# Whole 32-bit products in place of three split ones, in the projections and upward products of a second block

## The chip, the cores and the metric

The kernel runs on one core of one Trainium2 chip. The metric is the device time of one execution in microseconds (us), lower is better. Engines are named as in the profile: PE is the matrix engine (PEld its weight loads), DVE the vector engine, ACT the scalar engine, POOL is GpSimd, SP the engine whose queue issues most transfers.

## The reference, cut to what matters

One sequence of 256 tokens with 1024 channels goes through a first block (two layers of feed-forward, mixer, feed-forward), and then through a second block, whose mixer and experts follow. The change touches only the second block's mixer:

```python
h = modulate(rms_norm(x, g_pre_mix), shift, scale)      # 256 tokens x 1024 channels
z = h @ w_in + b_in                                     # 1024 -> 4736 columns: scans, attention, gates
y_att  = attention(...) @ w_up_att                      # 512 -> 1024
y_rwkv = scans(...)     @ w_up_rwkv                     # 512 -> 1024
x = x + norm((gate_a * y_att + gate_r * y_rwkv) @ w_out)
...                                                     # router, then 32 experts, four per token
```

All tensors are 32-bit floating point.

## The kernel before

The first block runs until about 1127 us of the span. The function `block2` is the second block up to the router, `experts` the rest. A framework orders the instructions of each engine at build time, from the order of the program and from planned durations; on the chip every engine keeps that order.

`norm` (L1370 to L1401) takes the two tiles of 128 tokens in turn: a factor per token, then eight products with a diagonal matrix (L1388) that scale and transpose at once, then DVE's modulation out of PSUM (L1391, tile `hch`), ACT's rounding into the float32r tile `hxH` (L1393), and DVE's remainder into `hxL` (L1394).

`Stream3` (L1135) brings the weights in 45 parts of 512 KB (37 for the projections, 8 for the upward products), 128 partitions by 1024 columns, read into two buffers `ws` (L1145). Each part is split in two halves of 512 columns: ACT rounds a half into `wh` (L1154), and the remainder `wl` is formed by DVE or, where the function `POOLED` says so, by GpSimd (L1156). Four pairs of halves are held, three halves ahead of use.

`pair` (L1403) forms 256 output columns from two parts: for each block of 128 columns and each 128 channels, three products of 128x128 weights with 256 tokens (L1412 to L1414), which are rounded weights with rounded input, rounded weights with the remainder of the input, and remainder of the weights with rounded input. There are 296 such triples. Five pairs come first (`first`: what the scans need). The other pairs (`fill`) are woven with the steps of the scans by the list `PACE`. A step of the scans in this stretch is either a feature step (products L260, L261, some twelve DVE operations from L264 to L296, then products L250 on `BKT`) or a part of the inverses of small triangular matrices (DVE, L320 to L340, 62 of them in a chain at L329 and L331, then products L346 to L356).

After them come attention, woven with the scans' chunks, then `rwkv_out`, then `up_att` and `up_rwkv`: `up` (L1566) is the same triple on the split outputs of attention (`atH`, `atL`, L1554 and L1555) and of the scans (`rwH`, `rwL`, L1623 and L1624), 64 triples at L1573 to L1575. The output product follows (L1666, whole 32-bit operands already), then router and experts. The experts' weights, 384 transfers of 1 MB (L1325), are read into 18 buffers.

Of the kernel before, what the change touches and what calls it, by code (L numbers as in the profile page):

```python
# [32 lines left out]
# buffers of the hidden units' chunks  # L33
NH = 4
N0 = 3
# steps of the scans beside each of the projections
PACE = [2] + [1, 2] * 4 + [1] * 6
# first ranks of an expert's groups of slots: 64, 32, 64, 64 and 32 of them
BASE = (0, 64, 96, 160, 224)
NWE, NWA = 18, 12  # L40
# subtiles of the last modulations read before the second mixer
PRE = 2
# subtiles of an expert in the order of their use: halves of the first product's rows one after the other, then the second's
ORDER = [0, 2, 4, 6, 1, 3, 5, 7, 8, 10, 9, 11]
# buffers of the second block's weights, of 512 KB
NRAW, NHI, AHEAD = 2, 4, 3


def POOLED(n, h):
    return (h or n % 2) and 10 <= n < 37 or n < 2  # L50
# columns of the per-layer channel pack of the first block
MC_CW, MC_CB, MC_G, MC_B, MC_LW, MC_LB, MC_BA, MC_BX, MC_LAM, MC_N = 0, 31, 32, 33, 34, 38, 39, 40, 41, 42
# columns of the channel pack of the second block
# [9 lines left out]
# subtiles of weights with a part of the split on GpSimd  # L63
# [3 lines left out]
def bc(ap, n, axis):  # L67
    """ap with a broadcast axis of n put in at position axis."""
    s = list(ap.shape)
    idx = [slice(None)] * len(s)  # L70
    idx.insert(axis, None)
    s.insert(axis, n)
    return ap[tuple(idx)].to_broadcast(s)
# [3 lines left out]
def program(ctx: ExitStack, tc: tile.TileContext, a, out, dbg=None, upto=99, only=None):  # L77
# [13 lines left out]
    # what is over before the experts  # L91
# [18 lines left out]
    def rstd_of(pool, var, eps, tag, more=None):  # L110
        """(var + more + eps) to the power of -1/2."""
# [12 lines left out]
    # ---------------------------------------------------------------- persistent  # L124
# [34 lines left out]
        # halves and sums of parameters that sit on the channels  # L159
# [11 lines left out]
    def normed_T(pool, bank, xt, mod, dst_h, dst_l):  # L171
        """rms norm, modulation and transposition of both token tiles, in two float32r parts."""
# [25 lines left out]
    def shifted(pads, ps, ch, dst):  # L198
        """Bias and token shift of a chunk, from PSUM to dst [P, 256]. ch counts the 15 shifted chunks."""
# [6 lines left out]
    def wkv(psb, k2, f, s_in, s_out, yT, kkn=None):  # L206
        """Chunked scans of both directions over chunks of 64 tokens, a piece at a time. Direction 0 keeps b on
        partitions 0-63 and k on 64-127 of what runs over tokens; direction 1 the other way round."""
# [17 lines left out]
        # k normalized  # L226
# [17 lines left out]
        def products(p, d):  # L244
            """Products of a (and r) with b and k inside a chunk."""
# [8 lines left out]
        for p in range(4):  # L254
            for d in range(2):
# [52 lines left out]
        # unit triangular inverses of the diagonal 32-blocks, one matrix on a partition  # L308
# [53 lines left out]
        # b, k and v with tokens on partitions  # L362
# [24 lines left out]
        # chunk after chunk, the heads in two halves  # L387
# [81 lines left out]
    def columns(ps, m, dst):  # L469
        """Modulations as columns: for each (tile, first of the two rows' groups) of dst."""  # L470
# [6 lines left out]
    def parts_of(split, dst):  # L477
        """What make_rows reads: two float32r parts of the rows that each (part, tile) of dst needs."""
# [9 lines left out]
    def make_rows(bank, parts, sel, dst):  # L488
        """Parts of x's modulation on all partitions, with the gains that go with them, for each (part, tile) of dst."""
# [8 lines left out]
    def context():  # L498
        """The modulation rows, and the keys, values and states of the context: three lists of steps that need
        no x, with the weights of each. The first two share what is in f."""  # L500
# [11 lines left out]
        def before():  # L512
            # the last part's first weights, for the norm behind the second mixer
# [61 lines left out]
        def mod_cols():  # L575
            # columns of shift and scale: 0 of x's first norm, 1 of the context's
# [76 lines left out]
    def weave(main, side, every):  # L653
        """The steps of main with one of side after every so many, and what is left of side at the end."""
# [41 lines left out]
    def proj(ps, w, j, n, xh, xl):  # L696
        """Chunk j of the n chunks of 128 columns of a subtile, [channels, tokens]."""
# [9 lines left out]
    def block1():  # L707
        KF, KM = 0.25 / ALPHA, 1.0 / ALPHA
        EPS = LN_EPS / (ALPHA * ALPHA)
        with ExitStack() as p1:  # L710
# [24 lines left out]
            def to_T(t, src):  # L735
                """x of a token tile, transposed, in two float32r parts."""
# [6 lines left out]
            def projx(ps, w, j, ts=slice(0, 2)):  # L743
                """Chunk j of the two of a subtile, of x's token tiles ts."""
# [61 lines left out]
            def rows(acc, w, h, l, first, last, ts=range(2)):  # L806
                """Products of a chunk of 128 rows of weights, [tokens, D]."""
# [8 lines left out]
            # ------------------------------------------------------------ gated unit  # L816
# [43 lines left out]
            # ------------------------------------------------------------ mixer  # L860
            def mixer(l):
# [3 lines left out]
                def consts_():  # L865
# [49 lines left out]
                def taps(g):  # L915
                    """The convolution of a half of the channels: first taps on GpSimd, the others on VectorE."""
# [180 lines left out]
            # ------------------------------------------------------------  # L1097
            st.xh, st.xl = parts("x")
            c0, c1, c2, before = context()
            # behind the ends of the units and mixers, what the norms there don't hold up  # L1100
# [33 lines left out]
    # =================================================================== phase 2  # L1134
    class Stream3:  # L1135
        """Parts of 512 KB of weights in the order of their use, read ahead and split into float32r parts,
        half a part at a time."""

        def __init__(self, raw, hl, ahead):
            self.raw, self.hl, self.ahead = raw, hl, ahead  # L1140
            self.srcs, self.f, self.t, self.n, self.i = [], {}, {}, 0, 0

        def load(self, i):
            self.f[i] = self.raw.tile([P, 1024], F32, name="ws", tag="ws")
            nc.sync.dma_start(self.f[i], self.srcs[i])  # L1145

        def ensure(self, i):
            while self.n < min(i + 1, 2 * len(self.srcs)):
                n, h = divmod(self.n, 2)
                if n not in self.f:  # L1150
                    self.load(n)
                f = self.f.pop(n)[:, 512 * h:512 * h + 512] if h else self.f[n][:, :512]
                hi = self.hl.tile([P, 512], F32R, name="wh", tag="wh")
                S.copy(hi, f)  # L1154
                lo = self.hl.tile([P, 512], F32R, name="wl", tag="wl")
# [4 lines left out]
        def next(self):  # L1160
            self.ensure(self.i + self.ahead)
            self.i += 1
            return self.t.pop(self.i - 1)
# [1115 lines left out]
```

## Time and profile before

| what | value |
|---|---|
| median of three runs | 2542.59 us (2541.45 to 2544.2) |
| span of the profiled execution, first to last instruction | 2534.9 us |
| own time of the profiled execution | not listed beyond its span; the median lies 7.7 us above it |
| mean granted PE clock | 0.945 of 2.4 GHz |
| PE, DVE, ACT, POOL busy | 2215.7, 1255.8, 766.8, 207.7 us |
| first block, second block to the router, experts | about 0 to 1127, 1127 to 1500, 1500 to 2535 us |

Busy times of PE count a matrix instruction from its start to its modelled end, so that instructions in a row overlap: the distance from one start to the next is what a stream of them costs.

### The profile page before, as it was taken

How to read it: one execution, taken by the hardware profiler on the slowest of the kernel's cores; microseconds unless marked ns; L12 is line 12 of the kernel's file. 1: busy time of each engine (PE TensorE's matmuls, PEld its weight loads, DVE VectorE, ACT ScalarE, POOL GpSimd, SP SyncE). 2: the span in 40 equal slices, each digit the busy share in tenths (PEclk: the TensorE clock that was granted, in tenths of full speed). 3: DMA queues.
4: the chain of work that ended last, by engine and by line, in shares of the span. 5: the costliest groups of instructions: out<-in, count | busy, mean ns of one | idle time of the engine just before them, and what ended most of it. 6: DMA issues, size and time to landing. Idle time of an engine off the chain costs nothing. (4 is left out here: it accounts for less than half of the span.)

```text
span 2534.9 us, 37664 instructions
## 1 busy us (share of the span) xinstructions
PE 2215.7 (87%) x15228; PEld 1562.4 (62%) x15228; DVE 1255.8 (50%) x2403; ACT 766.8 (30%) x1334; POOL 207.7 (8%) x198
## 2 busy tenths in 40 slices
PE   8999789999999789988879997887879778888787
PEld 7899668988997769978766743343333333333243
DVE  4667987886566975568985541111111112111112
ACT  3454354444444444446433311000101010000011
POOL 0001410001001410013430000000000000000000
PEclk9999899999999899999988998989999899999888
DMA  7655334444476355533320578969999999999983
GB/s 313 224 198 192 113 118 165 152 170 161 151 271 246 116 223 187 195 127 117 105 96 1 189 299 347 417 277 371 416 417 417 365 416 416 416 416 416 417 360 157
DMA packets 97081, 644.39 MB, mean 254 GB/s; under 512 B 11776, under 2 KB 13312, under 8 KB 23296
## 3 DMA queue, kind: packets, MB, share of 16 engines
q1 hardware_dynamic: 91152, 628.33, 63.7%
q10 hardware_dynamic: 5616, 11.75, 1.4%
q8 instruction: 213, 3.49, 0.6%
q14 instruction: 100, 0.82, 0.1%
HBM read 638.98 MB, written 1.05 MB: 252 GB/s over the span
## 5 line engine op out<-in xcount | busy, mean ns | idle before, releaser
L686 DVE TENSOR_TENSOR wl<-wst,wh 128x1024 fp32r<-128x1024 f32 x298 | 363.0, 1223 | 225.1 <-ACT wh L684 219.2
L751 PE MATMUL gu<-xh,wl 128*128 128x256 f32 x1632 | 458.2, 281 | 7.4 <-DVE wl L686 5.0
L749 PE MATMUL gu<-xh,wh 128*128 128x256 f32 x1632 | 459.9, 282 | 4.0 <-DVE yc L913 2.3
L750 PE MATMUL gu<-xl,wh 128*128 128x256 f32 x1632 | 458.2, 281 | 0.0
L684 ACT CAST wh<-wst 128x1024 fp32r<-128x1024 f32 x320 | 333.3, 1050 | 346.3 <-PE gu L750 188.8
L749 PEld LDWEIGHTS gu<-xh,wh 128*128 128x128 f32 x1632 | 311.1, 191 | 15.5 <-ACT xh L732 3.7
L751 PEld LDWEIGHTS gu<-xh,wl 128*128 128x128 f32 x1632 | 311.1, 191 | 12.0 <-DVE wl L686 6.6
L750 PEld LDWEIGHTS gu<-xl,wh 128*128 128x128 f32 x1632 | 311.2, 191 | 3.3 <-issue 0.3
L1805 PE MATMUL eg<-ew,eT 128*64 128x512 f32 x1024 | 267.9, 614 | 18.9 <-PEq L1988 12.1
L1849 DVE SCALAR_TENSOR_TENSOR eyl<-eg,gs,eyh 64x512 fp32r<-64x512 f32 x64 | 48.0, 750 | 358.4 <-ACT eyh L1848 358.4
L1866 PE MATMUL eg<-ew,xg 128*32 128x512 f32 x1408 | 184.2, 641 | 27.1 <-issue 20.4
L1805 PEld LDWEIGHTS eg<-ew,eT 128*64 128x64 f32 x1024 | 87.9, 140 | 170.4 <-issue 162.1
L1785 DVE TENSOR_SCALAR gg<-eg 128x256 f32<-128x256 f32 x42 | 17.8, 425 | 321.0 <-PE eg L1866 195.9
L1848 ACT ACTIVATE eyh<-eg,gs 64x512 fp32r<-64x512 f32 x64 | 43.7, 682 | 358.8 <-PE eg L1805 333.4
L1778 PE MATMUL eg<-ew,xg 128*64 128x512 f32 x640 | 147.1, 612 | 0.0
L1866 PEld LDWEIGHTS eg<-ew,xg 128*32 128x32 f32 x1408 | 47.7, 116 | 152.0 <-issue 135.4
L106 PE MATMUL acc<-wh,hl 128*128 128x512 f32 x352 | 138.8, 394 | 0.6 <-DVE hl L733 0.6
L105 PE MATMUL acc<-wl,hh 128*128 128x512 f32 x352 | 138.2, 393 | 0.0
L104 PE MATMUL acc<-wh,hh 128*128 128x512 f32 x352 | 138.0, 393 | 0.0
L1788 ACT ACTIVATE etu<-gg 128x256 f32<-128x256 f32 x45 | 18.8, 417 | 344.5 <-DVE gg L1785 324.9
L1761 PE MATMUL ms<-oh,hf 128*128 128x128 f32 (+2 forms) x608 | 85.4, 308 | 19.2 <-issue 13.4
L1414 PE MATMUL pj<-hxH,wl 128*128 128x256 f32 x296 | 88.9, 300 | 14.6 <-DVE wl L1156 13.2
(574 smaller groups left out, 3494.6 us busy)
## 6 DMA issues: line engine op xcount, KB each, us to landing
ew<-in_wexp SPq DMA_DIRECT2D x384, 1024.0 KB, 19.9
wst<-in_wgu SPq DMA_DIRECT2D x88, 1024.0 KB, 4.9
wst<-in_wd SPq DMA_DIRECT2D x44, 1024.0 KB, 4.9
wada<-in_wada SPq DMA_DIRECT2D x24, 1024.0 KB, 9.5
wst<-in_win SPq DMA_DIRECT2D x20, 1024.0 KB, 4.8
ws<-in_win SPq DMA_DIRECT2D x36, 512.0 KB, 3.6
wst<-in_wout SPq DMA_DIRECT2D x8, 1024.0 KB, 4.8
ws<-in_wup SPq DMA_DIRECT2D x8, 512.0 KB, 4.4
```

Of the source, the lines that this page charges most:

```text
L104: T.matmul(o, lh, rh, start=start, stop=False)
L105: T.matmul(o, lh, rl, start=False, stop=False)
L106: T.matmul(o, ll, rh, start=False, stop=stop)
L684: S.copy(hi, s_)
L686: (G if kind == SHARED and h else V).tensor_tensor(lo, s_, hi.bitcast(F32), op=ALU.subtract)
L749: T.matmul(o, h[:, c0:c0 + P], st.xh[:, ts, k], start=k == 0, stop=False)
L750: T.matmul(o, h[:, c0:c0 + P], st.xl[:, ts, k], start=False, stop=False)
L751: T.matmul(o, l[:, c0:c0 + P], st.xh[:, ts, k], start=False, stop=k == 7)
L1414: T.matmul(ps[:, j], l[:, c0:c0 + P], hh[:, kk], start=False, stop=kk == 7, skip_group_check=True)
L1778: T.matmul(ps[r][64 * j:64 * j + 64], xg[:, k], W(4 * r + 2 * j + q, k % 4), start=False, stop=k == 7, skip_group_check=True)
L1805: T.matmul(ps[c * two][64 * c:64 * c + 64], hT[:, r, j, b], W(8 + 2 * (c ^ flip) + k // 4, k % 4), start=k == 0, stop=k == 7)
L1866: T.matmul(ps[32 * b:32 * b + 32], xg[:, k], W(2 * b + q, k % 4), start=False, stop=k == 7, skip_group_check=True, tile_position=(0, 32 * b))
```

## The change

The splits are dropped. Weights are read into six buffers of 512 KB and used from there; the inputs are kept whole; each triple becomes one product with 32-bit operands. In `norm` every second chunk's modulation moves from DVE to ACT, and the results go straight into the input tile.

```diff
-NRAW, NHI, AHEAD = 2, 4, 3
-def POOLED(n, h):
-    return (h or n % 2) and 10 <= n < 37 or n < 2
+NRAW = 6
...
     class Stream3:
...
-                hi = self.hl.tile([P, 512], F32R, name="wh", tag="wh")
-                S.copy(hi, f)
-                lo = self.hl.tile([P, 512], F32R, name="wl", tag="wl")
-                (G if POOLED(n, h) else V).tensor_tensor(lo, f, hi.bitcast(F32), op=ALU.subtract)
-                self.t[self.n] = (hi, lo)
+        def load(self, n):
+            while self.n < min(n, len(self.srcs)):
+                self.t[self.n] = self.raw.tile([P, 1024], F32, name="ws", tag="ws")
+                nc.sync.dma_start(self.t[self.n], self.srcs[self.n])
                 self.n += 1
         def next(self):
-            self.ensure(self.i + self.ahead)
+            n, h = divmod(self.i, 2)
+            self.load(n + NRAW)
             self.i += 1
-            return self.t.pop(self.i - 1)
+            return self.t[n][:, 512 * h:512 * h + 512]
...
-        hh = hp.tile([P, 8, 256], F32R, name="hxH")
-        hl_ = hp.tile([P, 8, 256], F32R, name="hxL")
+        hx = hp.tile([P, 8, 256], F32, name="hx")
...
-                            V.tensor_scalar(f_[:, i], ps[:, i], modc[:, 0, 0, c:c + 1], modc[:, 0, 1, c:c + 1],
-                                            op0=ALU.mult, op1=ALU.add)
-                        S.copy(hh[:, cs, ts], f_)
-                        V.tensor_tensor(hl_[:, cs, ts], f_, hh[:, cs, ts].bitcast(F32), op=ALU.subtract)
+                            if i % 2:
+                                S.activation(hx[:, c, ts], ps[:, i], AF.Identity, scale=modc[:, 0, 0, c:c + 1], bias=modc[:, 0, 1, c:c + 1])
+                            else:
+                                V.tensor_scalar(hx[:, c, ts], ps[:, i], modc[:, 0, 0, c:c + 1], modc[:, 0, 1, c:c + 1],
+                                                op0=ALU.mult, op1=ALU.add)
...
-                        T.matmul(ps[:, j], h[:, c0:c0 + P], hh[:, kk], start=kk == j == 0, stop=False, skip_group_check=True)
-                        T.matmul(ps[:, j], h[:, c0:c0 + P], hl_[:, kk], start=False, stop=False, skip_group_check=True)
-                        T.matmul(ps[:, j], l[:, c0:c0 + P], hh[:, kk], start=False, stop=kk == 7, skip_group_check=True)
+                        T.matmul(ps[:, j], w[:, c0:c0 + P], hx[:, kk], start=kk == j == 0, stop=kk == 7, skip_group_check=True)
...
-                S.copy(at.h[:, :, ts], at.po)
-                V.tensor_tensor(at.l[:, :, ts], at.po, at.h[:, :, ts].bitcast(F32), op=ALU.subtract)
+                S.copy(at.x[:, :, ts], at.po)
...
-                        T.matmul(o[:, j], h[:, c0:c0 + P], yh[:, kk], start=kk == j == 0, stop=False, skip_group_check=True)
-                        T.matmul(o[:, j], h[:, c0:c0 + P], yl[:, kk], start=False, stop=False, skip_group_check=True)
-                        T.matmul(o[:, j], l[:, c0:c0 + P], yh[:, kk], start=False, stop=kk == 3, skip_group_check=True)
+                        T.matmul(o[:, j], w[:, c0:c0 + P], y[:, kk], start=kk == j == 0, stop=kk == 3, skip_group_check=True)
...
-                V.tensor_tensor(y, y, f.vT[:, c], op=ALU.mult)
-                S.copy(ro.h[:, c], y)
-                V.tensor_tensor(ro.l[:, c], y, ro.h[:, c].bitcast(F32), op=ALU.subtract)
+                V.tensor_tensor(ro.x[:, c], y, f.vT[:, c], op=ALU.mult)
...
-        for i in range(2):
-            st.load(i)
+        st.load(NRAW)
```

## Rows read from the trace of the kernel before

**Rows 1.** Stretches: length; busy PE, PEld, DVE, ACT, POOL; granted clock; DMA share; GB/s.

```profile
1134.30:1166.40 32.10, 31.88 (x241) 31.59 (x242) 25.31 (x38) 17.99 (x36) 7.38 (x5) 0.90 0.48 164
1166.40:1247.90 81.50, 68.34 (x500) 59.81 (x498) 73.01 (x144) 44.55 (x103) 36.22 (x34) 0.94 0.28 91
1247.90:1321.70 73.80, 55.18 (x595) 52.17 (x594) 64.65 (x93) 25.86 (x49) 27.25 (x23) 0.84 0.31 103
...
1413.90:1455.70 41.80, 38.88 (x278) 31.27 (x276) 24.57 (x44) 16.41 (x27) 1.27 (x3) 1.00 0.71 268
1455.70:1560.00 104.30, 91.73 (x423) 45.90 (x422) 35.19 (x116) 13.99 (x34) 4.70 (x6) 0.90 0.75 303
1560.00:2534.00 974.00, 791.37 (x4437) 342.38 (x4436) 172.88 (x496) 94.59 (x191) 7.65 (x23) 0.93 0.93 381
```

**Rows 2.** What SP's transfers waited for, 1120 to 1500 us (total, times, longest).

```profile
SPq L1325 <- PE wb L447: 99.7, 1, 99.7
...
SPq L1325 <- PE ac L1666: 16.7, 4, 5.7
```

**Rows 3.** What PE's instructions waited for, 1134 to 1322 us (total, times, longest).

```profile
PE wb L250 <- DVE BKT L292: 10.9, 6, 3.4
PE wb L346 <- DVE invL L339: 5.4, 1, 5.4
```

**Rows 4.** Groups of PE, 1166.4 to 1247.9 us, then 1247.9 to 1321.7 us.

```profile
L1414 PE MATMUL pj<-hxH,wl 128*128 128x256 f32 x108 | 31.4, 291 | 1.4 <-POOL wl L1156 1.4
...
L1414 PE MATMUL pj<-hxH,wl 128*128 128x256 f32 x109 | 34.0, 312 | 13.2 <-DVE wl L1156 13.2
```

**Rows 5.** Timeline of PE: third products of triples (start us, length us).

```profile
1139.96 0.41 PE L1414 MATMUL pj<-hxH,wl 128*128 128x256 f32 x1
...
1141.06 0.28 PE L1414 MATMUL pj<-hxH,wl 128*128 128x256 f32 x1
...
1142.13 0.28 PE L1414 MATMUL pj<-hxH,wl 128*128 128x256 f32 x1
```

**Rows 6.** Timeline of PE: whole 32-bit products, two instructions for each.

```profile
1360.06 0.59 PE L1561 MATMUL pj<-gl,g 128*128 128x256 f32 x2
...
1460.86 15.72 PE L1666 MATMUL ac<-ew,zg 128*128 128x512 f32 x36
```

**Rows 7.** Three source lines: all their durations in ns (min, median, max), first and last start.

```profile
L1561 PE MATMUL pj<-gl,g x8: 379/379/483, 1360.1 to 1394.5; 128*128 128x256 f32 x8
L1156 DVE TENSOR_TENSOR wl<-ws,wh x46: 673/685/2304, 1138.4 to 1451.8; 128x512 fp32r<-128x512 f32 x46
L291 DVE SCALAR_TENSOR_TENSOR BKT<-BKT,wk x16: 408/416/1517, 383.7 to 1245.9; 128x256 f32<-128x256 f32 x16
```

**Rows 8.** Timelines of DVE and of POOL, 1209 to 1213 us.

```profile
1209.99 1.52 DVE L291 SCALAR_TENSOR_TENSOR BKT<-BKT,wk 128x256 f32<-128x256 f32 x1
...
1209.93 4.12 POOL L1156 TENSOR_TENSOR wl<-ws,wh 128x512 fp32r<-128x512 f32 x3 [1.05 <-ACT wh L1154]
```

**Rows 9.** Groups of DVE, 1247.9 to 1321.7 us (busy us, mean ns).

```profile
L329 DVE TENSOR_TENSOR ttmp<-invL,invX 128x31 f32<-128x31 f32 (+15 forms) x31 | 18.4, 595 | 1.1
L331 DVE TENSOR_TENSOR invX<-invX,ttmp 128x31 f32<-128x31 f32 (+15 forms) x31 | 16.6, 535 | 0.9
```

**Rows 10.** The same operations in the first block's scan, 480 to 560 us.

```profile
L331 DVE TENSOR_TENSOR invX<-invX,ttmp 128x31 f32<-128x31 f32 (+15 forms) x31 | 10.6, 341 | 0.7
L329 DVE TENSOR_TENSOR ttmp<-invL,invX 128x31 f32<-128x31 f32 (+15 forms) x31 | 10.6, 341 | 0.7
```

**Rows 11.** Remainders (L1156) alone: busy on DVE, on POOL; clock, DMA share, GB/s.

```profile
1166.40:1247.90 81.50, 5.91 (x8) 28.80 (x20) 0.94 0.28 91
1247.90:1321.70 73.80, 7.55 (x11) 26.23 (x19) 0.84 0.31 103
```

**Rows 12.** Timeline of PE at the end of the norm.

```profile
1129.75 3.00 PE L1388 MATMUL wb<-dr,xf 128*128 128x128 f32 x16 [3.66 <-DVE dr L1381]
...
1134.30 0.58 PE L1412 MATMUL pj<-hxH,wh 128*128 128x256 f32 x1 [1.55 <-ACT hxH L1393]
```

More of the change, by code (lines that the diff above doesn't have):

```diff
@@ L1135, in program, with __init__ @@
     class Stream3:
[L1139 to L1152, printed above, removed]
-                hi = self.hl.tile([P, 512], F32R, name="wh", tag="wh")
-                S.copy(hi, f)
-                lo = self.hl.tile([P, 512], F32R, name="wl", tag="wl")
-                (G if POOLED(n, h) else V).tensor_tensor(lo, f, hi.bitcast(F32), op=ALU.subtract)
-                self.t[self.n] = (hi, lo)
+        def __init__(self, raw):
+            self.raw, self.srcs, self.t, self.n, self.i = raw, [], {}, 0, 0
+        def load(self, n):
+            while self.n < min(n, len(self.srcs)):
+                self.t[self.n] = self.raw.tile([P, 1024], F32, name="ws", tag="ws")
+                nc.sync.dma_start(self.t[self.n], self.srcs[self.n])
                 self.n += 1
         def next(self):
-            self.ensure(self.i + self.ahead)
+            n, h = divmod(self.i, 2)
+            self.load(n + NRAW)
             self.i += 1
-            return self.t.pop(self.i - 1)
+            return self.t[n][:, 512 * h:512 * h + 512]
     class Experts:
@@ L1344, in block2 @@
         kkn = yT = grow.rearrange("q (c t) -> q c t", c=4)
-        st = Stream3(ps_.enter_context(tpool(name="p2s", bufs=NRAW)), ps_.enter_context(tpool(name="p2l", bufs=NHI)), AHEAD)
+        st = Stream3(ps_.enter_context(tpool(name="p2s", bufs=NRAW)))
         psb = pa.enter_context(tpool(name="p2b", bufs=3, space=PSUM))
@@ L1383, in tile_ @@
                         ps = (psb if t else pjb).tile([P, 4, P], F32, name="wb" if t else "pj", tag="wb" if t else "pj")
-                        f_ = p.tile([P, 4, P], F32, name="hch", tag="hch", bufs=4)
-                        cs = slice(4 * q, 4 * q + 4)
                         for i in range(4):
@@ L1406, in pair @@
             for i in range(2 * n):
-                h, l = st.next()
+                w = st.next()
                 for j in range(n):
@@ L1499, in att_consts @@
             at.p = ap.enter_context(tpool(name="p2a", bufs=1))
-            at.h = at.p.tile([P, 4, 256], F32R, name="atH")
-            at.l = at.p.tile([P, 4, 256], F32R, name="atL")
+            at.x = at.p.tile([P, 4, 256], F32, name="atX")
             at.mask = at.p.tile([P, 2, P], F32, name="amask")
@@ L1564, in bonus, with up @@
             S.copy(f.vT[:, p], ps[:, 1])
-        def up(o, yh, yl):
+        def up(o, y):
             for i in range(2):
-                h, l = st.next()
+                w = st.next()
                 for j in range(2):
@@ L1572, in up @@
                         kk, c0 = 2 * i + k, 256 * k + P * j
-                        T.matmul(o[:, j], h[:, c0:c0 + P], yh[:, kk], start=kk == j == 0, stop=False, skip_group_check=True)
-                        T.matmul(o[:, j], h[:, c0:c0 + P], yl[:, kk], start=False, stop=False, skip_group_check=True)
-                        T.matmul(o[:, j], l[:, c0:c0 + P], yh[:, kk], start=False, stop=kk == 3, skip_group_check=True)
+                        T.matmul(o[:, j], w[:, c0:c0 + P], y[:, kk], start=kk == j == 0, stop=kk == 3, skip_group_check=True)
         def up_att(i):
             ps = pj()
-            up(ps, at.h, at.l)
+            up(ps, at.x)
             z = zg[:, 2 * i:2 * i + 2]
@@ L1594, in rwkv_out @@
             dump("yT", yT)
-            dump("atT", at.h.bitcast(F32))
+            dump("atT", at.x)
             mp = ro.p = ap.enter_context(tpool(name="p2r", bufs=1))
-            ro.h = mp.tile([P, 4, 256], F32R, name="rwH")
-            ro.l = mp.tile([P, 4, 256], F32R, name="rwL")
+            ro.x = mp.tile([P, 4, 256], F32, name="rwX")
             cs = [slice(2 * i, 2 * i + 2) for i in range(2)]
@@ L1621, in rwkv_out @@
                     V.scalar_tensor_tensor(y[:, j], y[:, j], at.lw[:, p:p + 1], f.bon[:, p], op0=ALU.mult, op1=ALU.add)
-                V.tensor_tensor(y, y, f.vT[:, c], op=ALU.mult)
-                S.copy(ro.h[:, c], y)
-                V.tensor_tensor(ro.l[:, c], y, ro.h[:, c].bitcast(F32), op=ALU.subtract)
-            dump("rwT", ro.h.bitcast(F32))
+                V.tensor_tensor(ro.x[:, c], y, f.vT[:, c], op=ALU.mult)
+            dump("rwT", ro.x)
         mg = Ctx()
@@ L1631, in up_rwkv @@
             ps = pj()
-            up(ps, ro.h, ro.l)
+            up(ps, ro.x)
             z, c = zg[:, 8 + 2 * i:10 + 2 * i], slice(2 * i, 2 * i + 2)
```

## The prediction

> **What bounds the kernel now.** I read the stretches first. In the experts, from 1560 us on, the transfers are busy 93% of the time and move 381 GB/s, while PE is busy for 791 of 974 us: that part is paced by the weights coming in. Between 1455.7 and 1560 us they run at 303 GB/s [rows 1]: their buffers are full and wait for use. The SP queue says the same. Its first transfer for the output product waits for the scans' last products (L447, 99.7 us), and later ones wait for buffers that the output product frees (L1666, 16.7 us) [rows 2]. So the experts' stream starts when the second block lets it, and has a length of its own. A microsecond gained or lost in the second block arrives at the end unchanged; this is the assumption under the sum.
>
> Inside the second block the change touches four stretches. I call them A (1134.3 to 1166.4 us, the first five pairs), B (to 1247.9, features of the scans beside pairs), C (to 1321.7, inverses beside pairs) and E (1413.9 to 1455.7, the upward products); between C and E lies attention. In A, PE is busy 31.9 of 32.1 us and is the bound. In B it is DVE, busy 73.0 of 81.5 us, with PE idle for 13.2; in C DVE again, 64.7 of 73.8, with PE idle for 18.6 [rows 1]. What ended PE's idle time is named: 10.9 us waited for `BKT`, DVE's last result of a feature step, 5.4 for the transposes after the inverses [rows 3], 13.2 for remainders from DVE and 1.4 for remainders from GpSimd [rows 4]. The reader should see that PE pays for DVE here, and that DVE is busy partly with work for PE.
>
> **What the change adds.** PE's price. At the high clock the third products of triples start at 1141.06 and, three triples on, at 1142.13: 0.357 us for a triple. Until 1140.8 us the clock stood at half, and the same product lasted 0.41 instead of 0.28 [rows 5]. A whole 32-bit product is two instructions. In the output product 36 of them with 512 columns take 15.72 us, 0.437 each; half the columns should take 0.218. L1561 has 256 columns: its two instructions take 0.59 us together, and one alone lasts 0.379, so 0.21 between their starts [rows 6, 7]. I take 0.43 us for a product of 256 columns, and 0.86 at half the clock (an estimate, twice that). Each triple replaced costs 0.43 - 0.357 = 0.07 us more: 296 in the projections 21 us, 64 upward 4.5 us.
>
> The Trainium skill (FP8 and Floating Point Precision, section TensorE Precision Notes) speaks against the change: it counts four passes through the array for a true 32-bit product, and a reduced form that truncates each operand. With passes of equal price that would be four thirds of the triple, 0.476 us, and 0.12 more for each of the 360 products, 43 us in place of 25. The rows of L1666 and L1561 lie below that, since a stream of float32r products costs more than its columns alone.
>
> **What it removes.** Of the 90 halves of weights, DVE forms 46 remainders at 0.685 us [rows 7], and GpSimd the rest. ACT, which rounds all of them, is busy less than 60% of A, B, C and E [rows 1], so what it saves gives nothing by itself. The remainders on GpSimd cost DVE as well: while three of them ran from 1209.93 to 1214.05 us, L291 took 1.52 us [rows 8], 1.1 more than its median of 0.416 [rows 7]. For the inverses the sum is clean, since the first block runs the same 62 operations without splits: 18.4 + 16.6 = 35.0 us here [rows 9] against 21.2 there [rows 10], so 13.8 us come back, beside 19 remainders on GpSimd. With the 11 remainders of its own, 7.6 us, DVE's 64.7 us in C fall to 43. In B 20 run on GpSimd [rows 11]; at 1.1 us each (L291's stretch) they cost DVE 22 us at most, at C's rate 14. Its own eight take 5.9 us, so DVE's 73 us fall to about 53.
>
> **The sum, stretch by stretch.**
> Norm and A. Now the transposing products end at 1132.75 us, and the first product starts at 1134.30, released by the rounding [rows 12]. Without rounding and with half of the evacuations on ACT the first channels are ready before the transposes end, so I start at 1132.8. The weights' first transfers still wait for the end of the first block, as before, and six buffers in place of two keep them ahead afterwards. The clock is at half until about 1140.8 [rows 5]: 8 us at 0.86 make 9.3 products, the other 70.7 at 0.43 take 30.4. A ends at 1171.2 instead of 1166.4: **+4.8**.
> B. PE was busy 68.3 us; 108 products [rows 4] add 7.6; the share of the lower clock (0.94 granted, 0.06 x 81.5 = 4.9 us lost, of which two thirds by its products) gives back 3.3: 72.6 us is the floor, above DVE's 53. Of the idle time 1.4 goes with its instruction; of the rest, 10.9 behind `BKT`, I keep 4, since every engine's order is fixed and a feature step still crosses three engines. 76.6 in place of 81.5: **-4.9**, between -8.9 (nothing kept) and +6.2 (all but the 1.4 kept, and the lower clock).
> C. PE was busy 55.2; 109 products add 7.6; the lower clock (0.84 granted, 11.8 us lost, of which I count half, since PE was partly idle then) gives back 5.9: 56.9. DVE's chain beside it is 43 us, then the last products and copies, so PE leads. I keep 4 of the 18.6 idle. 60.9 in place of 73.8: **-12.9**, between -16.9 and +7.6 (everything kept, the 13.2 now as waits on the inverses).
> Attention loses one remainder at its end, of the same size as L1156's 0.685 us: **-0.7**.
> E. 64 products add 4.5, and of the 2.9 idle [rows 1] I let 0.8 go, the waits for splits: **+3.7**. The rounding and remainder after the scans leave the path to `up_rwkv`, but the products of attention cover them.
> Together 4.8 - 4.9 - 12.9 - 0.7 + 3.7 = -10.0 us: a span of 2525 for 2534.9, and 2542.6 - 10.0 = 2532.6, rounded to **2532 us**, on the median, which lies 7.7 above the profiled span. The best sum, with nothing kept, is -18.0.
>
> **The rivals.**
> 1. *DVE's relief is half used.* PE keeps 16 us of its idle time in B and C instead of 8, and the sum is -2: about 2541 us. For it: orders are fixed at build time, and 10.9 + 5.4 of PE's idle microseconds [rows 3] were not for splits but for results of the scans. Against it: DVE now has 14 us of slack or more in each stretch, by the loads above.
> 2. *The scans wait for PE* (slower). PE runs in order, so a feature step's products stand behind whole pairs. A pair of 16 products now takes 6.9 us instead of 5.7. If each of the eight feature steps' two visits and the inverses' two come late by that and DVE starves meanwhile, PE keeps its 30 us idle and the lower clock, and the bounds above add to 4.8 + 6.2 + 7.6 - 0.7 + 3.7 = +21.6: 2564 us. It decides from the point where more than 18 us of the idle and slow-clock time stay. Against it: three buffers of features are in flight and DVE is no longer the busiest.
> 3. *Four passes at full price.* A product of 256 columns costs four float32r streams of 0.119, so 0.476 us: another 0.046 x 360 = 16.6 us on PE, the bound by then, so +6.6: 2549 us. For it only that neither row of whole products is a long stream with 256 columns; against it both rows. This is what the Trainium skill's rule above would give (FP8 and Floating Point Precision, section TensorE Precision Notes).
> 4. *The experts hide the difference.* If their stream already waited for nothing, the gain would vanish: 2542. The 303 GB/s before 1560 us [rows 1] speak against it; it shares the chance of rival 1.
>
> **How the numbers follow.** A measurement of this kernel can tell about 0.2%, 5 us. My forecast, any sum from -20 to -5, gets 0.72. Rivals 1 and 4 lie within 5 us: 0.13 together. Rival 2 gets 0.10 and rival 3 gets 0.05, slower together 0.15. The range reaches down to 2522, a little below the best sum in case attention gains from an earlier warm PE, and up to 2551, past rival 3, which leaves out most of rival 2; the forecast's own range is 2522 to 2537.
>
> **What would show it.** In the changed profile: products of 256 columns at 0.43 us in a run; A longer by 3 to 6 us; L291, L329 and L331 at 0.42, 0.34 and 0.34 us; waits of PE in B and C down from 31 us to under 10; the end of C near 1309 instead of 1321.7 us; the granted clock in B and C above 0.95; upward products some 4 us longer; experts of the same length. The prediction is wrong if PE's waits for `BKT` and the inverses grow, if the product costs near 0.48, or if the experts' stretch changes its length.

## The result, and the profile after

The changed kernel takes 2511.93 us (median of four runs, 2506.14 to 2515.28) against 2543.39 us for the kernel before on the same chip (four runs, 2541.45 to 2548.68): a ratio of 0.9886, 95% interval 0.9859 to 0.9913. The forecast was 2532 with a range from 2522 to 2551, so the sign was right, but the time lies below the range, and the gain is three times the one forecast. The profiled execution has a span of 2504.3 us, 30.6 less than before.

The stretches of the changed kernel, with the columns of [rows 1]: A, B and C; attention; the upward products to the first output product; from there to the experts' first product; the rest.

```profile
1134.70:1169.30 34.60, 34.60 (x163) 30.48 (x163) 9.62 (x20) 8.80 (x20) 1.89 (x1) 1.00 0.53 184
1169.30:1240.50 71.20, 68.65 (x386) 55.24 (x384) 53.86 (x136) 30.47 (x75) 9.13 (x14) 1.00 0.31 102
1240.50:1294.40 53.90, 53.90 (x489) 47.49 (x489) 44.14 (x82) 10.00 (x21) 1.52 (x4) 1.00 0.42 140
1294.40:1386.80 92.40, 85.94 (x916) 62.37 (x914) 53.72 (x138) 34.38 (x93) 7.30 (x6) 0.93 0.03 7
1386.80:1420.00 33.20, 33.20 (x141) 26.27 (x137) 13.30 (x23) 6.24 (x8) 0.31 (x2) 0.95 0.91 362
1420.00:1478.80 58.80, 53.84 (x175) 28.11 (x174) 19.76 (x59) 10.20 (x25) 4.38 (x5) 0.86 0.58 223
1478.80:2504.30 1025.50, 831.85 (x4697) 362.08 (x4696) 189.48 (x556) 100.05 (x203) 7.94 (x24) 0.93 0.92 378
```

The reader should see two things in the first three lines. PE is busy from end to end in A and C and idle for 2.5 us in B, where it was idle for 13.2 and 18.6 in B and C before; and its granted clock is 1.00 throughout, 2.4 GHz, where it was 0.90, 0.94 and 0.84 [rows 1]. DVE is busy for 53.86 and 44.14 us in B and C, 19 and 21 less. What PE still waits for between 1134 and 1295 us, where [rows 3] stood before:

```profile
PE wb L246 <- DVE BKT L288: 1.7, 2, 1.2
PE wb L256 <- ACT wk L259: 0.7, 1, 0.7
```

The two operations of the inverses, in the groups of DVE in C where [rows 9] stood, have the first block's durations again [rows 10]:

```profile
L327 DVE TENSOR_TENSOR invX<-invX,ttmp 128x31 f32<-128x31 f32 (+15 forms) x31 | 10.6, 343 | 1.1
L325 DVE TENSOR_TENSOR ttmp<-invL,invX 128x31 f32<-128x31 f32 (+15 forms) x31 | 10.6, 342 | 1.1
```

The line of `BKT` (L287 now), its durations in B, has lost its long cases [rows 7]:

```profile
L287 DVE SCALAR_TENSOR_TENSOR BKT<-BKT,wk x8: 409/412/417, 1183.9 to 1238.5; 128x256 f32<-128x256 f32 x8
```

For comparing all runs I cut the second block at PE instructions that every kernel has. "A+B" runs from the first projection product to the last product of a feature step, C to the scans' first transposing product, "att" to the first product of the norm behind the scans, E from there to the first output product (shorter than the prediction's E), F to the experts' first product, X to the end. Worked out from the starts of these instructions in each profile, in us (A+B and C as one sum in the column A-C):

| run | start | A+B | C | A-C | att | E | F | X | span |
|---|---|---|---|---|---|---|---|---|---|
| before | 1134.3 | 113.4 | 74.0 | 187.4 | 98.5 | 35.5 | 47.2 | 1032.0 | 2534.9 |
| c1_before_again | 1134.5 | 112.8 | 74.4 | 187.2 | 99.0 | 39.1 | 47.2 | 1031.6 | 2538.6 |
| after | 1134.7 | 105.5 | 54.2 | 159.7 | 92.4 | 33.2 | 58.8 | 1025.5 | 2504.3 |
| c2_after_again | 1136.9 | 105.7 | 54.2 | 159.9 | 98.4 | 31.5 | 58.5 | 1029.1 | 2514.3 |
| e1_gpsimd | 1139.5 | 112.6 | 64.0 | 176.6 | 96.4 | 33.6 | 58.8 | 1026.1 | 2531.1 |
| e2_dve | 1133.0 | 105.5 | 58.7 | 164.2 | 94.1 | 33.7 | 58.7 | 1019.6 | 2503.3 |
| e3_both | 1138.6 | 114.6 | 64.8 | 179.4 | 95.7 | 33.8 | 58.7 | 1026.3 | 2532.4 |
| e4_dve_all | 1140.7 | 110.4 | 68.3 | 178.7 | 95.8 | 37.2 | 46.8 | 1037.7 | 2536.8 |
| e7_nraw2 | 1134.9 | 108.5 | 56.6 | 165.1 | 91.4 | 43.5 | 45.5 | 1025.3 | 2505.6 |
| e9_rows_early | 1136.5 | 105.5 | 54.2 | 159.7 | 92.5 | 37.6 | 45.4 | 1024.4 | 2496.1 |
| c3_rows_early_again | 1139.2 | 105.6 | 54.2 | 159.8 | 95.7 | 37.6 | 45.4 | 1026.9 | 2504.5 |
| e10_no_remainders | 1138.3 | 96.1 | 56.3 | 152.4 | 94.2 | 30.1 | 51.3 | 1047.0 | 2513.2 |
| e11_unread | 1135.1 | 110.4 | 72.6 | 183.0 | 92.6 | 38.4 | 47.2 | 1048.5 | 2544.7 |
| e14_split_up | 1134.1 | 106.5 | 54.2 | 160.7 | 95.4 | 38.6 | 45.4 | 1028.8 | 2502.9 |

A-C repeats within 0.2 us for the same kernel and falls by 27.5 with the change. That is most of the gain; the other columns change too, some up and some down, and need care: att is 98.5 and 99.0 in the two profiles of the kernel before, 92.4 and 98.4 in the two of the changed one.

### The profile page after: what moved, and what is told of

It is laid out like the page before. It is cut to its first block, busy times and chain, and to the rows that moved or that the text cites. A ratio compares the mean times of both kernels' runs of the same rounds, so it can differ in the third digit from the quotient of the medians.

```text
span 2504.3 us, 36636 instructions
## 1 busy us (share of the span) xinstructions
PE 2216.4 (89%) x14868; PEld 1551.0 (62%) x14868; DVE 1187.8 (47%) x2341; ACT 718.4 (29%) x1246; POOL 145.1 (6%) x154
## 5 line engine op out<-in xcount | busy, mean ns | idle before, releaser
L1778 PE MATMUL eg<-ew,eT 128*64 128x512 f32 x1024 | 262.7, 604 | 21.7 <-PEq L1961 18.5
L1395 PE MATMUL pj<-hx,ws 128*128 128x256 f32 x592 | 130.8, 381 | 0.0
L1395 PEld LDWEIGHTS pj<-hx,ws 128*128 128x128 f32 x592 | 111.6, 190 | 16.9 <-issue 0.6
## 6 DMA issues: line engine op xcount, KB each, us to landing
ew<-in_wexp SPq DMA_DIRECT2D x384, 1024.0 KB, 19.9
```

The source lines that it names most:

```text
L1395: T.matmul(ps[:, j], w[:, c0:c0 + P], hx[:, kk], start=kk == j == 0, stop=kk == 7, skip_group_check=True)
L1778: T.matmul(ps[c * two][64 * c:64 * c + 64], hT[:, r, j, b], W(8 + 2 * (c ^ flip) + k // 4, k % 4), start=k == 0, stop=k == 7)
```

## The experiments

**Loads put back.** The question is what made A to C shorter: the work that left DVE, the work that left GpSimd, or that products no longer wait for remainders. Three kernels take the changed one and form the old subtractions again on the engines that had them, on weights alone (a weight minus itself) and with no reader; `pooled` is the rule of `POOLED`. The diff is that of e1_gpsimd; e2_dve takes (0, False) and e3_both all four values.

```diff
+        def extra(self, i):
+            while self.d < min(i + 1, 2 * len(self.srcs)):
+                n, h = divmod(self.d, 2)
+                f = self.t[n][:, 512 * h:512 * h + 512]
+                pooled = (h or n % 2) and 10 <= n < 37 or n < 2
+                if pooled in (1, True):
+                    lo = self.lo.tile([P, 512], F32R, name="wl", tag="wl")
+                    (G if pooled else V).tensor_tensor(lo, f, f, op=ALU.subtract)
+                self.d += 1
...
+            self.extra(self.i + 3)
```

> The changed kernel with the 44 subtractions that GpSimd ran for the splits put back, on weights alone and with nothing reading their results (a weight minus itself, into two buffers); products stay whole. Theory 1 (the change took the bound from VectorE to TensorE, which now sets A, B and C): B loses some of VectorE's 17 us of slack to the shared port and C 14 of its 10, so the time is 0 to 6 us above the changed kernel's, 2512 to 2518. Theory 2 (GpSimd's stretching of VectorE, 14 us in C and 14 to 22 in B, was by itself the time that came back): 20 us or more above it, 2532 and later. In both the inverses' operations last 0.5 to 0.6 us instead of 0.343.

Measured: ratio 0.9956 (0.9941 to 0.9972), 0.007 or 18 us above the changed kernel's 0.9886. C in this kernel, with the columns of [rows 1]:

```profile
1252.10:1316.10 64.00, 57.46 (x494) 50.27 (x491) 52.08 (x82) 10.25 (x21) 16.10 (x17) 0.92 0.33 116
```

What its PE waited for in B and C:

```profile
PE wb L246 <- DVE BKT L288: 6.9, 3, 2.9
PE wb L342 <- DVE invL L335: 5.0, 1, 5.0
PE wb L343 <- DVE invL L336: 1.6, 1, 1.6
```

And its groups of DVE in C that hold the inverses:

```profile
L325 DVE TENSOR_TENSOR ttmp<-invL,invX 128x31 f32<-128x31 f32 (+15 forms) x31 | 15.0, 483 | 1.1
L327 DVE TENSOR_TENSOR invX<-invX,ttmp 128x31 f32<-128x31 f32 (+15 forms) x31 | 14.5, 467 | 1.1
```

The subtractions among GpSimd's 17 instructions in C:

```profile
L1145 POOL TENSOR_TENSOR wl<-ws 128x512 fp32r<-128x512 f32 x13 | 14.9, 1156 | 17.2 <-DMA ws<-in_win 15.6 <-DMA ws<-in_win2z 1.6
```

These 13 subtractions make DVE's same 82 instructions last 52.1 us instead of 44.1, 0.61 us for each subtraction; the inverses, at 0.47 and 0.48 us, are stretched a little less than the 0.5 to 0.6 expected. The 8 us are less than DVE's slack of 10 us, and still C grows by 10: DVE's work here is a chain that PE waits for at one place (6.6 us before the products that take the transposed inverses), and C's clock is down to 0.92. So theory 1, which set the load against the slack, is wrong for GpSimd, and theory 2 is nearer, though its 20 us are not reached: GpSimd's 44 subtractions alone undo 16.9 of the 27.5 us of A-C.

> The changed kernel with VectorE's 46 subtractions for the splits put back on weights alone, with nothing reading their results; products stay whole. 0.685 us each: 5.9 us in B, 7.6 in C, the rest in A and the upward products. Theory 1 (TensorE sets A, B and C now and VectorE has slack): 0 to 4 us above the changed kernel. Theory 2 (VectorE's own splits were time of the path): 13 us or more above it, 2525.

Measured: ratio 0.9913 (0.9893 to 0.9933), some 7 us above the changed kernel with intervals that overlap; A-C grows by 4.5 us, all of it in C, where the clock is at 0.94. That is nearer theory 1, by the profile just above its 0 to 4 us: the 46 subtractions on DVE fit into slack, but those in C not quite.

> The changed kernel with all 90 subtractions for the splits put back on the engines that ran them, on weights alone, with nothing reading their results; products stay whole. VectorE then has before's load in B and C (73 and 64 us against 68 and 54 of TensorE). Theory 1 (bound moved to TensorE; VectorE is the bound again with both loads): B and C go back to about 81 and 74 us, A stays at 34.5: 2535 to 2550. Theory 2 (what came back is that the products no longer wait for remainders, not the load): B and C stay within 8 us of the changed kernel's 71 and 54, 2512 to 2520.

Measured: ratio 0.9976 (0.9961 to 0.9991), A-C 179.4. B is as theory 1 has it; C at 64.8 lies between the two:

```profile
1253.20:1318.00 64.80, 57.03 (x494) 49.96 (x491) 60.26 (x96) 10.26 (x21) 15.72 (x17) 0.92 0.32 115
```

Since nothing here has to wait for a rounding, the subtractions come at other times: in C GpSimd runs 13 of them against 19 before, DVE 15 against 11, and DVE's busy time there is 60.3 us against 64.7 [rows 1]. So the load in C is lighter than before's. That leaves open whether the last 9 us of C (64.8 to 74) were waits for remainders; e11_unread below tests it.

**The kernel before, edited.** First all remainders on DVE:

```diff
 def POOLED(n, h):
-    return (h or n % 2) and 10 <= n < 37 or n < 2
+    return False
```

> The kernel before, with all 90 remainders on VectorE and none on GpSimd; splits and triples as before. VectorE gets 20 more remainders in B and 19 in C of 0.685 us, 13.7 and 13.0 us, and loses the stretch by GpSimd's port, 14 to 22 and 14 us by my sum in the prediction. If the stretch is as large as that sum: within 5 us of the kernel before, 2538 to 2548. If the stretch was smaller than the remainders that it spares VectorE (half of it): 10 to 15 us slower, 2553 to 2558.

Measured: ratio 0.9966 (0.9946 to 0.9987), 8.6 us faster than before; A-C 178.7, also 8.6 less. Neither number of the expectation: GpSimd's share of the splits cost more than it spared. The groups of DVE in C of this kernel:

```profile
L1156 DVE TENSOR_TENSOR wl<-ws,wh 128x512 fp32r<-128x512 f32 x31 | 21.0, 683 | 4.3 <-ACT wh L1154 4.2
L331 DVE TENSOR_TENSOR invX<-invX,ttmp 128x31 f32<-128x31 f32 (+15 forms) x31 | 10.6, 341 | 0.7
L329 DVE TENSOR_TENSOR ttmp<-invL,invX 128x31 f32<-128x31 f32 (+15 forms) x31 | 10.6, 340 | 0.6
```

The durations of the inverses are those of [rows 10] with no remainder on GpSimd, although DVE itself forms 31 remainders. What slowed them in [rows 9] was the engine beside, not the load.

Then the remainders formed as before, but not read, and not formed at all. In both the third product reads the rounded weights, so the remainders of the weights are left out of the result. The router, fed by it, chooses differently (PE runs 4878 instructions in X, 4696 in every other run), and the experts take longer (X of 1047 and 1048.5). So of these two only the stretches up to the experts can be compared, not their ratios of 1.0060 (e11_unread) and 0.9932 (e10_no_remainders).

e11_unread:

```diff
-                self.t[self.n] = (hi, lo)
+                self.t[self.n] = (hi, hi)
```

e10_no_remainders:

```diff
-                lo = self.hl.tile([P, 512], F32R, name="wl", tag="wl")
-                (G if POOLED(n, h) else V).tensor_tensor(lo, f, hi.bitcast(F32), op=ALU.subtract)
-                self.t[self.n] = (hi, lo)
+                self.t[self.n] = (hi, hi)
```

> The kernel before with all 90 remainders formed on the same engines, but not read: the third product of each triple reads the rounded weights again, so the remainders are left out of the result. Load of VectorE and GpSimd as before, price of products as before; only TensorE's wait for remainders is gone (14.6 us in the profile of before, nearly all in C). Theory 1 (in C the wait for remainders is a cost of its own, as in the run with all subtractions put back unread, where C took 64.8 us against 74.0): C 62 to 66 us, B within 3 us of before's 81, 8 to 14 us faster than before. Theory 2 (load alone sets C, the wait only names where it shows): C within 3 us of 74, within 4 us of before.

Measured: C 72.6 against 74.0, A-C 183.0 against 187.3. PE's waits in C:

```profile
PE wb L346 <- DVE invL L339: 11.6, 1, 11.6
PE pj L1412 <- ACT wh L1154: 5.3, 2, 4.9
```

Theory 2, by C. The 13.2 us that PE waited for DVE's remainders [rows 4] did not go away with their reader: they moved to the inverses, 11.6 us instead of the 5.4 of [rows 3] (7.4 in c1_before_again), and to the rounding. The row of a wait named where PE stood, not what made it late. What makes up the 8 us between this C and that of e3_both is not separated. The load is heavier here (DVE busy for 64.2 us against 60.3), the halves wait for their roundings, and PE's cheaper products may reach the waits sooner.

> The kernel before without the 90 remainders of weights: the third product of each triple reads the rounded weights again, so the remainders of the weights are left out of the result. VectorE and GpSimd then have no more to do than in the changed kernel (ACT still rounds), and a product costs 0.357 us instead of 0.432. Theory 1 (in the changed kernel TensorE's price sets A, B, C and E): A, C and E shorter than in the changed kernel by 5, 8 and 4 us and B by 3 to 8, so 15 to 25 us faster than it, 2487 to 2497. Theory 2 (the scans' own chain stands right behind TensorE): B and C stay within 3 us of the changed kernel's 71 and 54 and only A and E gain, 6 to 10 us faster than it.

Measured: A 29.7 us (the changed kernel 34.6), B 66.4 (71.2), C 56.3 (54.2), E 30.1 (33.2). C of this kernel:

```profile
1234.40:1290.70 56.30, 49.22 (x600) 48.55 (x598) 44.58 (x82) 25.89 (x49) 1.20 (x4) 0.91 0.39 137
```

What its PE waited for in C:

```profile
PE wb L346 <- DVE invL L339: 5.5, 1, 5.5
PE wb L347 <- DVE invL L340: 1.6, 1, 1.6
```

Theory 1 for A, B and E, theory 2 for C. A cheaper product would save 4.9, 4.8 and 3.1 us there, so the price of the whole product is on the path, at somewhat less than the forecast's 0.07 us times the count (5.6, 7.6 and 4.5). In C it buys nothing: 8 us less work for PE turn into 7.1 us of waiting for the inverses and a clock of 0.91. The dearer product hides the whole chain of the inverses.

This run also takes the gain apart. Without the remainders alone A-C falls from 187.3 to 152.4 us, though ACT still rounds all 90 halves; PE waits for none of these roundings, so by themselves they held nothing up. The changed kernel, with the dearer products, gives 7.3 of these 34.9 us back, and some 27.5 are left.

**Two buffers instead of six.**

```diff
-NRAW = 6
+NRAW = 2
```

> The changed kernel with two buffers of 512 KB for the second block's weights, as many as held them before ahead of the splits, in place of six. A buffer feeds eight products, 3.46 us; a transfer of 512 KB takes 3.7 us or more from issue to landing in the profile of the changed kernel. Theory 1 (the six buffers are a needed part of the change: a whole weight is held until its last product, while a split freed its buffer early): 1 to 2.5 us of wait for each of the ten buffers of A and for most of C's, with the lower clock behind them, 15 to 40 us slower than the changed kernel. Theory 2 (the weights come far ahead anyway): within 4 us of it.

Measured: ratio 0.9901 (0.9876 to 0.9927), A-C 5.4 us longer, the time about 4 us above the changed kernel with intervals that overlap. That is theory 2, at its edge. PE's wait for the weights between 1134 and 1301 us is:

```profile
PE pj L1395 <- DMA ws<-in_win: 2.8, 4, 1.7
```

The expectation's 3.7 us for a transfer was too long: those of 512 KB take 3.1 to 8.4 us in the profile of the changed kernel, with a median of 3.5. Most of the change's gain doesn't rest on the six buffers. The planner also placed the row products differently here (E 43.5, F 45.5), which gives 1 to 3 us back and led to the next pair of runs.

**The row products.** F is 11.6 us longer after the change, and no step of the prediction has it. PE's timeline there:

```profile
1427.71 1.12 PE L1640 MATMUL ac<-ew,zg 128*128 128x512 f32 x2
1431.32 1.17 PE L491 MATMUL tp<-mhl,onesel 32*128 32x512 f32 x2 [2.49 <-ACT bon L492]
1432.42 2.08 PE L1640 MATMUL ac<-ew,zg 128*128 128x512 f32 x2
1434.42 1.22 PE L491 MATMUL tp<-mhl,onesel 32*128 32x512 f32 x2
1435.57 2.08 PE L1640 MATMUL ac<-ew,zg 128*128 128x512 f32 x2
1437.58 1.22 PE L491 MATMUL tp<-mhl,onesel 32*128 32x512 f32 x2
```

L491 spreads the modulation rows over all partitions, 16 products that the diff doesn't touch. Before, the planner had put 12 of them between the upward triples; after, 14 stand behind the first output product. One waits 2.5 us for ACT's copy of an earlier result, and after the wait the output products (two instructions each) take 2.08 us instead of 1.12: the granted clock is at half until 1441.6 us. The next kernel writes them between attention's and the scans' upward products:

```diff
-        steps += weave(ups, ...)
-        steps += [([], rows_of), ([], open_sum)]
+        ups.insert(4, ([], rows_of))
+        steps += weave(ups, ...)
+        steps += [([], open_sum)]
```

> The changed kernel with the 16 products that spread the modulation rows (L491) written between the upward products of attention and those of the scans, in place of behind both; nothing else. In the changed kernel they stand among the first output products, wait 2.5 us for the copies of their results and leave the clock at half for 10 us: from the first output product to the first product of the experts 58.8 us against 47.2 before. Theory 1 (that stretch is on the path): it returns to 47 to 51 us while the upward products grow by about 5, 3 to 7 us faster than the changed kernel. Theory 2 (the transfers for the experts set the end; from the first output product to the end the kernels so far took 1078 to 1085 us whatever the stretch): what the stretch loses the experts gain, within 2 us of the changed kernel.

Measured: ratio 0.9868 (0.9840 to 0.9896); F 45.4, E 37.6, X 1024.4. Theory 1 by the profile, E and F together 83.0 instead of 92.0 with no gain of X lost; but the interval overlaps the changed kernel's. So it was timed again, beside the changed kernel on one chip, with the kernel before profiled once more.

> The changed kernel, unchanged, profiled and timed once more beside the next two. A and B together 105.5, C 54.2, from the first output product to the first product of the experts 58.8 us, each within 1.5 us; ratio to before 0.986 to 0.991.

Measured: 0.9883 (0.9855 to 0.9911), median 2511.58; A and B 105.7, C 54.2 and F 58.5, as expected; E and F together 90.0.

> The changed kernel with the 16 row products between the upward products, as in the earlier run, once more on the same chip as the changed kernel itself. Theory 1 (the half clock and the wait among the output products cost time at the end): 3 to 8 us faster than the changed kernel here too. Theory 2 (the experts' transfers absorb it): within 2 us.

F of this kernel, with the columns of [rows 1]; its clock is 0.92 where the changed kernel's F has 0.86:

```profile
1432.30:1477.60 45.30, 43.20 (x161) 24.96 (x159) 18.66 (x55) 7.95 (x21) 4.66 (x6) 0.92 0.61 234
```

Measured: 0.9836 (0.9808 to 0.9863), median 2498.83, 12.7 us less than the run beside it; E and F 83.0 again. All six times of this kernel (2497.32 to 2506.26) lie below all six of the changed one (2506.41 to 2516.12). Theory 1: F is on the path. The gain is larger than the 3 to 8 us expected; the profiles show 7 to 9 us of it in E and F, and how much of the rest is real the intervals don't tell. This is the fastest kernel of the study.

> The kernel before, unchanged, profiled once more, to see which stretches repeat. If the length of a stretch belongs to the kernel, A and B together take 113, C 74 and the stretch of attention 98.5 us within 2 us. If attention's 98.5 was a phase of the clock, it lies between 91 and 97 as in all other profiles so far, and attention's 6.1 us between the two kernels are no effect of the change by themselves.

Measured: A+B 112.8, C 74.4, att 99.0. All three repeat, so the kernel before was not caught in a bad phase; but the changed kernel's attention came out at 92.4 and 98.4 with the same PE waits and granted clocks of 0.93 and 0.86. A difference of 6 us there is not shown to come from the change.

**Upward products as triples again**, with the row products early; ACT rounds the halves, DVE forms the remainders.

```diff
-                        T.matmul(o[:, j], w[:, c0:c0 + P], y[:, kk], ...)
+                        T.matmul(o[:, j], h[:, c0:c0 + P], yh[:, kk], ...)
+                        T.matmul(o[:, j], h[:, c0:c0 + P], yl[:, kk], ...)
+                        T.matmul(o[:, j], l[:, c0:c0 + P], yh[:, kk], ...)
...
-NRAW = 6
+NRAW = 4
```

> The kernel with the row products early, and the 64 upward products as 192 float32r products of split weights and inputs again (ACT rounds, VectorE forms all 16 remainders, GpSimd none), with four buffers of 512 KB and two of each part; the projections stay whole. Theory 1 (TensorE is the bound in the upward products): 64 times 0.075 us, 3 to 5 us off E, 2 to 5 us faster than the run beside it. Theory 2 (the wait for the rounding and remainder after the scans comes back with it): E gains under 1 us.

Measured: ratio 0.9881 (0.9852 to 0.9910), about 10 us slower than the run beside it; E 38.6 against 37.6. PE's waits in E:

```profile
PE pj L1568 <- ACT wh L1144: 2.0, 1, 2.0
PE pj L1570 <- DVE wl L1146: 0.9, 1, 0.9
```

Theory 2: 4.8 us less of products, by the prices 0.075 us apart, is eaten by 3 us of waits for roundings and remainders and by the clock, 0.91 in E where it is 1.00 in the run beside it. Only 1.0 of the 10 us is in E; the profiles show 0.9 more in A+B and 1.9 in X, and the rest is not accounted for. The same for the first five pairs was not tried.

## Why the prediction was wrong in size

**What bounds the kernel** was read rightly. PE paid for DVE in B and C; with the splits gone PE is the bound in A, B and C, and A-C's 27.5 us arrive at the end. That the experts' part keeps its length did not hold (below).

**The price** was right: A holds 80 products and the 163 instructions in it take 34.60 us, 0.43 a product. Rival 3 is out: its 0.476 would make A 38.1. The Trainium skill (FP8 and Floating Point Precision, section TensorE Precision Notes) counts four passes for a true 32-bit product; four times the 0.119 us of a float32r stream is an estimate of 0.476 us, and the row lies a tenth below it.

**DVE's relief** was right: 53 and 43 us were forecast, 53.86 and 44.14 measured, the inverses 21.2 as forecast. The Trainium skill (SBUF — State Buffer, section SBUF: two separate sides) says that DVE's operations with two inputs in SBUF and GpSimd's that read SBUF exclude one another for a whole instruction. The runs agree in kind (0.341 us alone, 0.483 beside GpSimd, 0.595 in the kernel before). The mean cost to DVE of a subtraction on GpSimd is 7.9 / 13 = 0.61 us in e1_gpsimd and, by the inverses, 13.8 / 19 = 0.73 in the kernel before.

**The step that failed is the sum of B and C**, -4.9 and -12.9 forecast, -10.3 and -19.9 measured (B from 81.3 to 71.0 and C from 74.0 to 54.2 by the PE instructions named above). That is 12.4 of the 20.6 us by which the span came out shorter than the forecast's; of the others, attention's 5.4, the experts' 6.5 and A's 1.9 go the same way and E with F 5.6 the other way. The mechanism, PE paying for a late DVE, was right; two terms of the sum were mis-sized.
- *Kept idle time*: 4 us in each stretch, measured 2.5 in B and nothing in C, so 5.5 us too much was kept. The reason given, a fixed order and steps that cross three engines, was no reason for a fixed remainder of waits. Those for `BKT` and the inverses were 1.7 us and none; they grow when DVE is late again (6.9 and 6.6 us in e1_gpsimd), and they come back in C without any load when PE's products are cheaper (7.1 us in e10_no_remainders). So it took both, a faster DVE and PE's dearer products, to hide them.
- *The clock's give-back*: 3.3 and 5.9 counted, on the ground that PE was partly idle at the lower clock. PE's floors of 72.6 and 56.9 us came out as 68.65 and 53.90, 7.0 less together for the same 217 products (three of them moved from B to C). If all of that is the clock, 16.2 of the 16.7 us that the lower clock was reckoned to cost (4.9 and 11.8) came back; the same kernel's C lost 15.6 instead of 11.8 in c1_before_again, so this is no exact share.

The two belong together, and the runs show it in C: where PE is idle for longer, more time is lost by the granted clock (one minus the clock, times the length). It is no fixed rate: e2_dve and e7_nraw2 have the same idle time and lose 3.5 us and nothing.

| kernel | C, us | PE idle, us | granted clock | lost by the clock, us |
|---|---|---|---|---|
| after | 53.9 | 0 | 1.00 | 0 |
| e2_dve | 58.7 | 1.0 | 0.94 | 3.5 |
| e7_nraw2 | 56.5 | 1.1 | 1.00 | 0 |
| e1_gpsimd | 64.0 | 6.5 | 0.92 | 5.1 |
| e3_both | 64.8 | 7.8 | 0.92 | 5.2 |
| e10_no_remainders | 56.3 | 7.1 | 0.91 | 5.1 |
| e4_dve_all | 68.3 | 15.4 | 0.83 | 11.6 |
| c1_before_again | 74.4 | 16.6 | 0.79 | 15.6 |
| before | 73.8 | 18.6 | 0.84 | 11.8 |
| e11_unread | 72.6 | 17.6 | 0.80 | 14.5 |

**A** was forecast to start at 1132.8 and end at 1171.2; it started at 1134.7 and ended at 1169.3. The start didn't move earlier, so no gain from the shorter way through `norm` shows; the half clock that was assumed until 1140.8 us was over by the first product. In the kernel before A's clock was 0.90 and 0.94 in two profiles, and 1.00 in e11_unread, so this is no sure effect of the change.

**Attention and E**: -0.7 and +3.7 forecast. The step for E priced the products and missed that the planner, with other instructions to place, moves ones that the diff doesn't touch: E and F together grew by 9.3 us (6.5 by the means of two profiles each), and e9_rows_early and c3_rows_early_again show where: in F. Of attention's -6.1 nothing is shown to be the change's.

**The experts** were forecast at the same length. X is 1031.6 to 1037.7 in the three profiles with the kernel before's products (without e10 and e11), and 1019.6 to 1029.1 in the nine with whole projections. A longer E and F hiding part of X is no explanation, since the kernels with the row products early have E and F as short as before's and X as short as the changed one's. The gain lies between the experts' 300th and 1200th PE instruction, the same ones in both kernels (11.4 us; the rest of X is 4.9 us longer). Before, then after:

```profile
1570.00:1761.20 191.20, 157.72 (x904) 69.22 (x897) 34.88 (x106) 16.75 (x35) 0.94 (x3) 0.89 0.87 355
1547.00:1726.80 179.80, 148.20 (x905) 66.19 (x897) 34.36 (x105) 16.75 (x35) 0.93 (x3) 0.94 0.92 379
```

PE is idle for about as long (33.5 and 31.6 us), but before, its clock is lower and the transfers pause for longer: none lands from 1674.7 to 1697.5 us, in the changed kernel from 1650.1 to 1667.8. This stretch takes 191 to 193 us in before, c1_before_again, e4_dve_all and e14_split_up, and 178 to 182 in the eight with whole upward products. So in these profiles it goes with the upward products, not with the projections; no run here tests why, and the cause stays open.

**The rivals.** Rival 1 (relief half used), rival 2 (scans wait for PE) and rival 4 (experts hide it) are out by PE's waits in the profile after, by the clock of 1.00 and by the time. The sum of the terms by the means of two profiles each: A-C -27.5, attention -3.4, E and F +6.5, X -4.5, start +1.4, together -27.5, against -29 to -31 in the timed medians. That attention and the experts came out shorter, and E and F longer, is no credit to the forecast: none of the three was foreseen.

## What to carry to other kernels

Where one engine does work for another, what comes back when that work goes is the wait, the neighbour's slowing of the engine that stays, and the time that the lower clock took beside PE's waits. A, B and C here say that a stretch in which PE becomes busy from end to end should be costed near the full clock with hardly any idle time kept, and the caution put into the range; E, also busy throughout, had 0.95, since its first 3 us were at half the clock. A wait's row names where PE stood: take the reader away in thought and ask where it would stand next. And after an edit with a planned order, look for what the planner moved: 16 untouched products cost 7 to 9 us here until they were put in place by hand.

## What the runs showed of the hardware

- Moving subtractions from DVE to GpSimd made the kernel slower: all 90 on DVE is 8.6 us faster than 44 of them on GpSimd. A subtraction of 128x512 takes DVE 0.683 us, and one on GpSimd costs DVE 0.61 to 0.73 us by the stretching of other instructions alone.
- A whole 32-bit product with 256 columns costs 0.43 us in a stream, a triple of float32r products 0.357 us; with the splits on other engines the dearer one won by 27.5 us over the same three stretches.
- One wait of PE of 2.5 us among the output products was followed by 10 us at half the clock.
